# Layer B's queries by a seven-product block scheme, with the first tokens' z, k and v ahead of them

## The chip, the cores and the metric

The kernel runs on one core of one Trainium2 chip. A core has TensorE (PE, matmuls; PEld is its weight loads), VectorE (DVE), ScalarE (ACT), GpSimd (POOL) and SyncE (SP, which here issues most DMAs). The metric is the device time of one execution in microseconds, as the median of several runs.

## The reference

A hybrid decoder of two layers on 1024 tokens of width 1024, all in float32. Layer A is a gated MLP in chunks; layer B is sliding-window attention with 16 query heads, 4 key and value heads, ALiBi and sinks. Cut to what layer B computes:

```python
kv_in = rms_norm(h, kv_norm_g)
k_shared = (kv_in @ w_k).reshape(bsz, s_len, N_KV_HEADS, HEAD_DIM)
v_shared = (kv_in @ w_v).reshape(bsz, s_len, N_KV_HEADS, HEAD_DIM)
q, z = jnp.split(rms_norm(h, b_pre_g) @ w_in, 2, axis=-1)
q = q * (HEAD_DIM ** -0.5)
# per block of 128 queries: logits against the block's and the previous block's keys, + alibi, masked
m = jnp.maximum(jnp.max(logits, axis=-1), sink)
p = jnp.exp(logits - m[..., None])
denom = jnp.sum(p, axis=-1) + jnp.exp(sink - m)
o = jnp.einsum('bkgts,bskd->btkgd', p, vb) / denom
y = (o * jax.nn.silu(z)) @ w_out
h = h + rms_norm(y, b_post_g)
```

## The kernel before

**Numbers in two parts.** Each float32 operand of a large matmul is split into a high part in fp32r and a low part, the difference (`split` and `split_scaled`, L104 to L110): ACT writes the high part, DVE the low one. `mm3` (L168) then makes three matmuls: high by high, high by low, low by high. A product of one 128x128 weight tile with 512 tokens is thus three PE instructions, on L169 to L171.

**Stages.** The first tokens are 0 to 511 (h = 0), the second 512 to 1023 (h = 1). In order of time: the v layer of A; its u and z (`uz_layer`, the tiles ub, uc, ua, uz_slots); its output (`out_layer`); then layer B from L1204 on. A's three matrix products are already computed as seven block products for eight, with tiles T[1] to T[7] for the token side.

**Layer B.** q of the first tokens is computed first (`q_phase`, 8 output tiles of 128 by 8 tiles of K, in two passes of four PSUM banks), with the end of A for the second tokens (`chain_a`) as side work. Then k and v (`kv_phase`), with the transposes of the second tokens beside them (`norm_h1`); then z (`z_phase`). The first attention is `attn(0, ...)`: eight units (a block of 128 queries by half of the heads), each with two groups of scores (L1050), maximum (L1055, L1061), exponentials (L1065), normalising (L1070, L1071), transposes (L1078, L1079), causal selects on POOL (L1082, L1083), the product with v (L1097, L1099) and the gate (L1103). Between these, at four places for each unit, it draws steps from a generator of other PE work, the fill: 64 steps of k, v, q and half of z for the second tokens. A step is six matmuls of 512 columns, or their like. The second attention is filled with the other half of z and the output projections (`out_b0`, `out_b1`).

**Weights.** One object (`Weights`, L112) holds the order of all of layer B's weight tiles. A tile is loaded two steps ahead into one of three raw buffers by SP, and split one step ahead (L109 on ACT, L110 on DVE) into one of two pairs.

**What sets the order.** The framework orders each engine's instructions: program order is the priority, and an instruction goes when its operands and buffers are expected to be free. Waits are put in by it. Each DMA queue works in the order of issue.

**Other lines that matter below.** `broadcast_rstd` (L272) makes the token scale with two float32 matmuls on L278, from diagonal tiles. The first weight is loaded on ACT's queue (L406), behind the gains (L87). `evac` in `q_phase` (L971, L972) scales q out of PSUM and splits it into two half tiles.

## Time and profile before

| | |
|---|---|
| median of 3 runs | 1051.75 us (1051.14 to 1052.2) |
| the profiled execution | 1051.56 us, span 1049.8 us |
| instructions | 13661, of these 4994 matmuls |
| granted TensorE clock | 0.998 |
| HBM read, written | 125.21 MB, 31.46 MB |

The span is what the profile covers, from the first instruction to the last; the execution's own time holds 1.8 us more around it. A row of instructions gives the line, the engine, the operation, output and inputs by tile name, shape and count, then busy time, the mean of one in ns, and the idle time before it with what ended it. A row of the timeline begins with its start and its duration.

### The profile page before, as it was taken

What the parts mean: (1) busy time and instruction counts of PE and PEld (TensorE: products, weight loads), DVE (VectorE), ACT (ScalarE), POOL (GpSimd) and SP (SyncE); (2) the same over time, 40 slices, a digit from 0 to 9 for tenths busy, and PEclk for the clock granted to TensorE, in tenths of its full rate; (3) what the DMA queues carried; (4) which work ended last, traced back from release to release, by engine and by line L of the source; (5) the groups of instructions that cost most, each with busy time, mean ns of one, the idle gap of its engine ahead of it and who ended that gap; (6) DMA issues with size and microseconds to landing.
All of it is one profiled execution on the core that took longest, in us unless ns stands there. A gap on an engine that the chain in (4) does not pass through costs nothing.

```text
span 1049.8 us, 13661 instructions
## 1 busy us (share of the span) xinstructions
PE 1039.2 (99%) x4994; PEld 854.8 (81%) x4994; DVE 731.9 (70%) x1244; ACT 577.2 (55%) x989; POOL 195.2 (19%) x153
## 2 busy tenths in 40 slices
PE   9999999999999999999999999999999999999997
PEld 7888788888888888888888888888888777877776
DVE  6997466867768668677697587665247776667763
ACT  6683444555465565555444464654466665786631
POOL 0300003253342542530200000100001111011120
PEclk9999999999999999999999999999999999999999
DMA  8877252334333333347897642532222121211363
GB/s 310 271 282 269 101 177 88 116 105 143 124 121 116 132 124 117 108 137 272 322 352 270 201 160 93 200 102 86 95 81 71 51 81 61 81 61 61 121 220 120
DMA packets 80899, 157.56 MB, mean 150 GB/s; under 512 B 5824, under 2 KB 32704, under 8 KB 80832
## 3 DMA queue, kind: packets, MB, share of 16 engines
q1 hardware_dynamic: 76176, 147.75, 41.2%
q10 hardware_dynamic: 4656, 8.94, 2.4%
q8 instruction: 39, 0.64, 0.3%
q14 instruction: 28, 0.23, 0.1%
HBM read 125.21 MB, written 31.46 MB: 149 GB/s over the span
## 4 chain that ended last, share of the span: by engine, by line
PE 93%; DVE 4%; ACT 1%; issue 0%; DMA 0%; POOL 0%; DVEq 0%; POOLq 0%; ACTq 0%
PE ob L169 6%; PE ub L169 6%; PE ub L171 6%; PE ob L171 6%; PE ob L170 6%; PE ub L170 6%; PE qz L169 5%; PE qz L171 5%; PE qz L170 5%; PE uc L169 3%; PE uc L171 3%; PE uc L170 3%; PE s L1050 3%; PE sp L614 3%; PE vb L170 2%; PE vb L171 2%
## 5 line engine op out<-in xcount | busy, mean ns | idle before, releaser
L110 DVE SCALAR_TENSOR_TENSOR wlo<-raw_w,gn,whi 128x512 fp32r<-128x512 f32 x80 | 58.7, 758 | 62.2 <-ACT whi L109 62.0
L169 PE MATMUL qz<-n_hi,whi 128*128 128x512 f32 x256 | 101.0, 394 | 0.4 <-DVE q_lo L972 0.4
L171 PE MATMUL qz<-n_hi,wlo 128*128 128x512 f32 x256 | 100.0, 391 | 1.2 <-DVE wlo L110 1.2
L170 PE MATMUL qz<-n_lo,whi 128*128 128x512 f32 x256 | 99.8, 390 | 0.0
L109 ACT ACTIVATE whi<-raw_w,gn 128x512 fp32r<-128x512 f32 x80 | 54.9, 716 | 54.2 <-PE qz L170 35.0
L1065 ACT ACTIVATE pr<-pr,mx 128x129 f32<-128x129 f32 x128 | 50.0, 393 | 40.1 <-DVE mx L1061 40.0
L169 PEld LDWEIGHTS qz<-n_hi,whi 128*128 128x128 f32 x256 | 48.0, 188 | 16.6 <-issue 6.5
L105 ACT ACTIVATE uzhilo_g<-f 128x1024 fp32r<-128x1024 f32 x31 | 32.9, 1060 | 48.6 <-PE uc L171 42.7
L171 PEld LDWEIGHTS qz<-n_hi,wlo 128*128 128x128 f32 x256 | 48.0, 188 | 12.3 <-DVE wlo L110 2.1
L170 PEld LDWEIGHTS qz<-n_lo,whi 128*128 128x128 f32 x256 | 48.1, 188 | 9.3
L106 DVE TENSOR_TENSOR uzhilo_g<-f,uzhilo_g 128x1024 fp32r<-128x1024 f32 x31 | 39.0, 1257 | 19.9 <-ACT uzhilo_g L105 19.9
L209 ACT ACTIVATE uz_slots<-ub 128x512 f32<-128x512 f32 x48 | 28.3, 590 | 42.4 <-PE ub L171 39.0
L169 PE MATMUL ub<-T,whi_g 128*128 128x512 f32 x128 | 50.7, 396 | 0.0
L169 PE MATMUL ub<-T,uzhilo_g 128*128 128x512 f32 x128 | 50.5, 395 | 0.0
L171 PE MATMUL ub<-T,wlo_g 128*128 128x512 f32 x128 | 49.9, 390 | 0.0
L171 PE MATMUL ub<-T,uzhilo_g 128*128 128x512 f32 x128 | 49.9, 390 | 0.0
L170 PE MATMUL ub<-T,uzhilo_g 128*128 128x512 f32 x128 | 49.8, 389 | 0.0
L170 PE MATMUL ub<-T,whi_g 128*128 128x512 f32 x128 | 49.8, 389 | 0.0
L169 PE MATMUL uc<-T,uzhilo_g 128*128 128x512 f32 x124 | 48.9, 395 | 0.0
L170 PE MATMUL uc<-T,uzhilo_g 128*128 128x512 f32 x124 | 48.3, 389 | 0.0
L171 PE MATMUL uc<-T,uzhilo_g 128*128 128x512 f32 x124 | 48.3, 389 | 0.0
L105 ACT ACTIVATE whi_g<-raw_uz 128x1024 fp32r<-128x1024 f32 (+1 forms) x31 | 26.5, 854 | 36.7 <-PE ub L170 15.6
(332 smaller groups left out, 3071.4 us busy)
## 6 DMA issues: line engine op xcount, KB each, us to landing
raw_uz<-in_wuz_in_dram SPq DMA_DIRECT2D x32, 512.0 KB, 3.4
raw_w<-in_wqz_dram SPq DMA_DIRECT2D x32, 512.0 KB, 3.5
td<-uz_slots SPq DMA_DIRECT2D x56, 256.0 KB, 2.2
orawP2a<-td SPq DMA_DIRECT2D x28, 512.0 KB, 4.0
raw<-in_wv_in_dram SPq DMA_DIRECT2D x17, 512.0 KB, 4.8
vg<-vd SPq DMA_DIRECT2D x8, 1024.0 KB, 5.4
orawP2b<-in_wo_a_dram SPq DMA_DIRECT2D x16, 512.0 KB, 7.7
vraw<-in_wv_in_dram SPq DMA_DIRECT2D x13, 512.0 KB, 4.4
```

The lines of the kernel that those rows point to most:

```text
L105: nc.scalar.activation(hi, src, AF.Copy)
L106: nc.vector.tensor_tensor(lo, src, hi.bitcast(F32), ALU.subtract)
L109: nc.scalar.activation(hi, src, AF.Copy, scale=g)
L110: nc.vector.scalar_tensor_tensor(lo, src, g, hi.bitcast(F32), ALU.mult, ALU.subtract)
L169: nc.tensor.matmul(out, lhsT=a_hi, rhs=b_hi, start=start, stop=False, skip_group_check=True)
L170: nc.tensor.matmul(out, lhsT=a_hi, rhs=b_lo, start=False, stop=False, skip_group_check=True)
L171: nc.tensor.matmul(out, lhsT=a_lo, rhs=b_hi, start=False, stop=stop, skip_group_check=True)
L209: nc.scalar.activation(out, a, AF.Copy)
L614: nc.tensor.matmul(psv[:, n], lhsT=d["vg"][:, 4 * j + n, i * P:(i + 1) * P], rhs=d["wc"], start=True, stop=True)
L1050: nc.tensor.matmul(pss[par][:, g, w0:256], lhsT=q[par][:, m, bs_], rhs=w[par][:, p, ks], start=g + k == 0, stop=g + k == 2, skip_group_che ...
L1065: nc.scalar.activation(pr[:, i], pr[:, i], AF.Exp, bias=mx[:, i:i + 1], scale=-1.0, accum_out=dn[:, i:i + 1])
```

## The change

- **q in seven products.** The 1024 output channels of q are four groups of 256. Per group the weight is a 2 x 2 of blocks (two output tiles by two halves of K), the tokens a 2 x 2 (two halves of K by first and second tokens). Seven products of 12 matmuls each (4 tiles of K by three parts) replace eight, for both halves of the tokens at once. The token sums T[4] to T[7] are formed in `norm_sums`, beside z, k and v of the first tokens, which now come first. Products 1 and 2 of all four groups (`early_products`) need the first tokens alone; then come products 6, 5, 7, 3 and 4 of each group (`late_products`), with the weight sums in `prep1`.
- **Through DRAM.** The memory for this (pool `qp`) is that of attention, which is opened later. So z, k and v of the first tokens, the scaled weights and all of q are stored to DRAM (`zd`, `kd`, `qwd`, `qd`) and loaded again; q is split after the reload (`reload_q`), piece by piece, a step after its load (`reloads`).
- **Attention.** q is no longer fill. The first attention has 32 steps, six of them ahead of it (`first=6`, then 26). Half of the normalising goes to POOL, as four instructions of 128x128 for each unit.
- **Elsewhere.** `broadcast_rstd` uses fp32r in two parts, four matmuls; the first load moves to SP's queue, ahead of the x tiles; q of the first tokens takes tile P3, so the last output weights take P3 too.

The diff, cut to its core:

```diff
-            self.order += q + kv + z + kv + q + z
+            self.order += z + kv + kv + z
...
-            dg = sum_tile(f"dg{h}")[:, 0:512].rearrange("p (a b) -> p a b", a=4)
+            dg = st.tile([P, 2, 4, P], F32R, tag="xt", name=f"dg{h}")
             for j in range(4):
-                nc.vector.tensor_scalar(dg[:, j], ident, rx[h][:, j:j + 1], None, ALU.mult)
+                r = rx[h][:, j:j + 1]
+                nc.scalar.activation(dg[:, 0, j], ident, AF.Copy, scale=r)
+                nc.vector.scalar_tensor_tensor(dg[:, 1, j], ident, r, dg[:, 0, j].bitcast(F32),
+                                               ALU.mult, ALU.subtract)
             ps = bank("s", f"bc{h}")
-            nc.tensor.matmul(ps, lhsT=ones, rhs=dg.rearrange("p a b -> p (a b)"), start=True, stop=True)
+            for i in range(2):
+                nc.tensor.matmul(ps, lhsT=ones_r, rhs=dg[:, i].rearrange("p a b -> p (a b)"),
+                                 start=i == 0, stop=i == 1)
...
+        r0 = raws.take("v0")
+        load(r0[:, 0:512], wv_in[0, 0][:, 0:512])
         xload(xa[:, 0], 0, 0, 0, 1)
-        r0 = raws.take("v0")
-        nc.scalar.dma_start(out=r0[:, 0:512], in_=wv_in[0, 0][:, 0:512])
...
+    def norm_sums(n, yo, first):
...
+                split(n[0][:, ks, ts_], n[1][:, ks, ts_], ps)
+                if kq == 0:
+                    add(t1, ps, n_0[0][0][:, :, ts_].bitcast(F32), ALU.subtract)
+                    add(t1, t1, n_0[1][0][:, :, ts_].bitcast(F32), ALU.subtract, nc.gpsimd)
+                else:
+                    add(t3[:, :, ts_], ps, n[0][:, 0:HT, ts_].bitcast(F32), ALU.subtract)
+                    add(t2, ps, t1, ALU.subtract)
+                    add(t4, n_0[0][1][:, :, ts_].bitcast(F32), t2, ALU.subtract, nc.gpsimd)
+                    add(t3[:, :, ts_], t3[:, :, ts_], n[1][:, 0:HT, ts_].bitcast(F32), ALU.subtract, nc.gpsimd)
+                    add(t4, t4, n_0[1][1][:, :, ts_].bitcast(F32), ALU.add, nc.gpsimd)
+                yield
+            for m, src in ((5, t1), (6, t2)):
+                split(T[m][0][:, :, ts_], T[m][1][:, :, ts_], src)
+                yield
+            split(T[4][0][:, :, ts_], T[4][1][:, :, ts_], t4)
+            yield
...
+        def early_products(self):
+
+            for q in range(4):
+                self.prep_early(q + 1)
...
+                b = bank("mm", f"qa{q}")
+                self.product(q, 1, b, True, False)
+                self.p1[q] = sum_512(1 + q // 2, f"qp1_{q}")
+                copy(self.p1[q], b)
+                self.product(q, 2, b, False)
+                c = self.slot()
+                copy(c, b)
+                self.store(q, 0, 0, c)
+                yield
...
+        def late_products(self, side):
...
+                self.prep2(q)
+                self.load(q + 1)
...
+                step(side)
+                self.product(q, 6, b, True, False)
+                add(c01, p1, b, ALU.add)
+                self.product(q, 5, cc, True, False)
+                self.product(q, 7, b, False, False)
+                self.prep1(q + 1)
...
+                add(c11, p1, b, ALU.add)
+                add(c11, c11, cc, ALU.add)
+                self.store(q, 1, 1, c11)
+                self.product(q, 3, cc, False)
+                add(c01, c01, cc, ALU.add)
+                self.store(q, 0, 1, c01)
...
+                self.product(q, 4, b, False)
+                add(c10, p1, b, ALU.add)
+                self.store(q, 1, 0, c10)
...
+    def reload_q(q, i, r):
+
+        ms = slice(2 * i, 2 * i + 2)
+        for par in range(2):
+            rw, ot = half[par], half[1 - par]
+            g = qsc[rw, i // 2:i // 2 + 1]
+            nc.scalar.activation(q[par][rw, ms], r[rw], AF.Copy, scale=g)
+            nc.vector.scalar_tensor_tensor(q[par][ot, ms], r[rw], g, q[par][rw, ms].bitcast(F32),
+                                           ALU.mult, ALU.subtract)
...
+            if gp == 1:
+                nc.vector.reciprocal(dn[:, 0:4], dn[:, 0:4])
+                for i in range(4):
+                    nc.gpsimd.tensor_scalar(pr[:, i, 0:P], pr[:, i, 0:P], dn[:, i:i + 1], None, ALU.mult)
...
-            dn, pv = self.dn, self.pr[:, :, 0:P]
+            dn, pv = self.dn[:, 4:8], self.pr[:, 4:8, 0:P]
...
+    drain(qt.early_products())
+    q0, q1 = pair("P3", "q0"), None
+    side = reloads(0, None, None, 0, 1, None, 2, 3)
+    qt.late_products(side)
+    qp_ctx.close()
+    bp = ctx.enter_context(tc.tile_pool(name="bp", bufs=1))
...
+    reload_kv(qt.k0)
+    for i in range(4):
+        nc.sync.dma_start(out=z0[i // 2][:, i % 2 * 2:i % 2 * 2 + 2], in_=zd[i])
...
+    fill = chain(kv_phase(1, n1), z_phase(1, n1, z1, 0, 4))
+    attn(0, q0, z0, fill, 26, first=6,
+         side=chain(side, reloads(1, 0, 1)))
```

More of the change, by code (lines that the diff above doesn't have):

```diff
@@ L130, in split @@
         def split(self, i):
-            while len(self.done) <= min(i, len(self.order) - 1):
+            while len(self.done) <= min(i, self.limit - 1):
                 n = len(self.done)
@@ new lines, in reload_q, with reloads @@
+    def reload_q(q, i, r):
[6 more added lines that the diff above has]
+                                           ALU.mult, ALU.subtract)
+    def reloads(h, *pieces):
+        r = None
+        for i, p in enumerate(pieces + (None,)):
+            last = r
+            if p is not None:
+                r = raw_tile(f"q{h}_{p}").rearrange("p (m t) -> p m t", m=2)
+                nc.sync.dma_start(out=r, in_=qd[h][p])
+            if i and pieces[i - 1] is not None:
+                reload_q((q0, q1)[h], pieces[i - 1], last)
+            yield
@@ L979, in evac, with z_phase @@
+    def z_phase(h, n, z, m0, m1, keep=False):
         def evac(m, ps):
@@ L1104, in values, with attn @@
             split(q[0][:, ms, bs_], q[1][:, ms, bs_], yt)
-    def attn(h, q, z, fill, total, late=0):
+    def attn(h, q, z, fill, total, late=0, first=0, side=iter(())):
         taken = [0, 0]
+        for _ in range(first):
+            step(fill)
         n = 34 if late else 40
@@ L1123, in attn @@
             more()
+            step(side)
             if 0 <= i - 1 < len(units):
@@ new lines, in tile_yoco @@
+    main = chain(z_phase(0, n0, z0, 0, 8, keep=True), kv_phase(0, n0))
+    qt = QTiles()
+    step(main, main)
+    for i, _ in enumerate(main):
+        if i < 6 or i % 5 != 1 and i % 5 != 3:
+            step(side)
+        if i == 38:
+            qt.load_early(0)
+            qt.load_early(1)
+        elif i == 42:
+            qt.prep_early(0)
+            qt.load_early(2)
+    gp = post_gain(b_post, "gpb")
+    drain(side)
+    drain(qt.early_products())
+    q0, q1 = pair("P3", "q0"), None
@@ L1230, in tile_yoco @@
     fill = chain(z_phase(1, n1, z1, 4, 8), tail())
-    attn(1, q1, z1, fill, 48, 2)
+    attn(1, q1, z1, fill, 48, 2, side=reloads(1, 2, 3))
     drain(fill)
```

244 lines of the change are left out of this document (179 added, 65 removed).

## The prediction

> **What bounds the kernel now.** I read the page first: the busy times, then the chain that ended last.
>
> ```profile
> PE 1039.2 (99%) x4994; PEld 854.8 (81%) x4994; DVE 731.9 (70%) x1244; ACT 577.2 (55%) x989; POOL 195.2 (19%) x153
> ...
> PE 93%; DVE 4%; ACT 1%; issue 0%; DMA 0%; POOL 0%; DVEq 0%; POOLq 0%; ACTq 0%
> ```
>
> TensorE (PE) is busy 99% of the span and is 93% of the chain. A busy PE is not PE at its peak, since the matmuls overlap, so I read its price per matmul from the starts in the timeline: a product removed is worth its pitch, not its duration.
>
> Then the windows, cut at the stages around the change (start:end, length, then busy time and count of PE, PEld, DVE, ACT and POOL, granted clock, DMA share, GB/s). 654 to 699 is q of the first tokens, 699 to 726 their k and v, 726 to 769 their z, 769 to 892 the first attention; the first row is a piece of the v layer.
>
> ```profile
> 20.00:62.00 42.00, 41.66 (x183) 33.79 (x182) 40.90 (x48) 28.07 (x39) 10.20 (x3) 1.00 0.75 257
> ...
> 654.00:684.00 30.00, 28.88 (x127) 23.25 (x125) 21.95 (x32) 18.34 (x32) 3.82 (x3) 1.00 0.51 178
> ...
> 699.00:726.00 27.00, 27.00 (x182) 24.80 (x181) 17.26 (x27) 14.65 (x26) 0.00 (x0) 1.00 0.26 79
> 726.00:769.00 43.00, 43.00 (x192) 35.58 (x191) 14.21 (x21) 19.88 (x31) 0.00 (x0) 1.00 0.30 98
> 769.00:892.00 123.00, 122.56 (x669) 97.45 (x668) 90.63 (x254) 78.91 (x212) 15.29 (x14) 1.00 0.20 65
> 892.00:997.00 105.00, 105.00 (x547) 81.64 (x546) 72.38 (x222) 73.28 (x199) 16.15 (x14) 1.00 0.25 81
> ```
>
> PE fills each of these stages to within 1.2 us. In the first attention it can, because q of the second tokens is fill there: VectorE (DVE) has 90.6 us of work, but 123 us to do it in. That cover is what the change takes away.
>
> **The matmuls removed.** The timeline of PE in the present q gives the pitch; 54 matmuls lie between these two rows:
>
> ```profile
> 654.10 0.39 PE L169 MATMUL qz<-n_hi,whi 128*128 128x512 f32 x1
> ...
> 666.34 0.39 PE L169 MATMUL qz<-n_hi,whi 128*128 128x512 f32 x1
> ```
>
> (666.34 - 654.10)/54 = 0.2267 us. q is now 2 x 8 x 8 x 3 = 384 matmuls of this shape. Afterwards it is 4 groups x 7 products x 4 k x 3 = 336. So 48 x 0.2267 = **10.9 us** less, all on the path. The Trainium skill's page "TensorE: Matmul & The Clock Gate", section "Back-to-back issue gap", gives about 131 ns for a sustained matmul of 512 columns with its weight load; by that the 48 would be worth an estimated 6.3 us. The trace does not agree, and its pitch decides.
>
> **Smaller gains.** The broadcast of rstd, the start of the kernel, and three PE waits behind q's evacuation:
>
> ```profile
> 105.92 1.88 PE L278 MATMUL bc<-dg,ones 128*128 128x512 f32 x4
> ```
> ```profile
> 0.80 0.86 SPq L307 DMA_DIRECT2D xa<-in_xT_dram  x2
> ...
> 1.24 0.45 ACTq L406 DMA_DIRECT2D raw_v<-in_wv_in_dram  x1
> ...
> 5.78 1.24 POOL L415 CAST whi_v<-raw_v 128x512 fp32r<-128x512 f32 x2 [5.28 <-DMA raw_v<-in_wv_in_dram]
> ```
> ```profile
> 682.57 0.50 PE L171 MATMUL qz<-n_hi,wlo 128*128 128x512 f32 x1 [0.66 <-DVE wlo L110]
> ...
> 684.12 0.51 PE L171 MATMUL qz<-n_hi,wlo 128*128 128x512 f32 x1 [0.59 <-DVE wlo L110]
> ...
> 836.47 0.48 PE L169 MATMUL qz<-n_hi,whi 128*128 128x512 f32 x1 [0.45 <-DVE q_lo L972]
> ```
>
> The broadcast's two float32 matmuls show as four passes of 1.88 us together; four passes in fp32r at 0.227 are 0.91: **1.0 us** gained. The first load is issued 0.44 us after SP's first, behind the gains on ACT's queue; first on SP's it lands up to that much earlier, at the cost of the x loads, which it delays by as much; between 0 and 0.44 I take **0.4**, since the row after it waits for exactly this load. The three waits (0.66 + 0.59 + 0.45 = **1.7 us**) go with the work that jams DVE there. Gains: 10.9 + 1.0 + 0.4 + 1.7 = 14.0 us.
>
> **Waits inside the products.** An early group adds its second product to the bank from which ACT has just to copy the first; a late group's product 3 goes into the bank that DVE reads only after product 7, in two additions. PE waits if nothing else is at hand. The copies and additions from PSUM now cost:
>
> ```profile
> L209 ACT ACTIVATE uz_slots<-ub 128x512 f32<-128x512 f32 x48 | 28.3, 590 | 42.4 <-PE ub L171 39.0
> ...
> L206 DVE TENSOR_TENSOR uz_slots<-uz_slots,uc 128x512 f32<-128x512 f32 x32 | 22.0, 687 | 18.5 <-PE uc L171 11.3 <-ACT uz_slots L209 6.8
> ```
>
> With some 0.25 us for the last matmul's end, uncovered that is 4 x (0.59 + 0.25) = 3.4 us early and 4 x (2 x 0.69 + 0.25) = 6.5 us late: 9.9 us. The lower bound is 0. The order on PE is not the program's: here fill is put between the matmuls of one score, which the program issues together:
>
> ```profile
> 803.20 0.28 PE L1050 MATMUL s<-kh,q_hi 128*128 128x256 f32 x1
> ...
> 803.31 0.39 PE L169 MATMUL qz<-n_hi,whi 128*128 128x512 f32 x1
> ...
> 806.08 0.28 PE L1050 MATMUL s<-kl,q_hi 128*128 128x256 f32 x1
> ```
>
> So the next group's product, whose weights are split a group ahead, can be put into such a gap. I take **1.5 us**, near the lower end, by these rows.
>
> **z, k and v with the sums beside them.** Per block of tokens there are three more subtractions and three more splits on DVE, 24 in all, and 16 instructions on POOL:
>
> ```profile
> L106 DVE TENSOR_TENSOR n_lo<-nt,n_hi 128x512 fp32r<-128x512 f32 x8 | 5.1, 685 | 0.7 <-ACT n_hi L105 0.7
> ```
> ```profile
> L206 POOL TENSOR_TENSOR uz_slots<-uz_slots 128x512 f32<-128x512 f32 x17 | 27.7, 1631 | 0.5
> ```
>
> 24 x 0.685 = 16.4 us of DVE go into 70 us of PE, where the windows from 699 to 769 show DVE at 31.5 of 70; POOL gets 16 x 1.63 = 26 us. Both fit; I take nothing. Without that cover it would be the splits' waits, some 0.6 us each as in the two rows at 682 and 684.
>
> **From the last product to the first score.** Keys' tiles lie on memory that the products free last. The chain: addition 0.69, store of the last block, memset of kl, then four copies and a split of k; on SP the reloads of z and v (2.5 MB) and q's pieces stand ahead of the second tokens' third weight.
>
> ```profile
> td<-uz_slots SPq DMA_DIRECT2D x56, 256.0 KB, 2.2
> ```
> ```profile
> L1013 POOL MEMSET kl<- 64x2048 f32 x2 | 4.0, 2008 | 22.8 <-DVE ohiloP0b L106 19.1 <-DVE hb L763 3.8
> ```
> ```profile
> L1017 ACT ACTIVATE kh<-pk 64x512 fp32r<-64x512 f32 x4 | 2.4, 594 | 0.6 <-PE pk L171 0.5
> ```
>
> 0.69 + 2.2 + 2.0 + 4 x 0.59 = 7.3 us in a row, against six steps of fill put first, 6 x 6 x 0.227 = 8.2 us. Covered it costs 0; with ACT's queue full (eight copies, 4.7 us, and a weight's split) some 4 us. I take **1.0**.
>
> **The first attention with half its fill.** PE: 122.6 - 192 x 0.2267 = 79.0 us. DVE, from the groups of 769 to 892:
>
> ```profile
> L110 DVE SCALAR_TENSOR_TENSOR wlo<-raw_w,gn,whi 128x512 fp32r<-128x512 f32 x32 | 23.9, 772 | 13.9 <-ACT whi L109 13.9
> ...
> L1071 DVE TENSOR_TENSOR pr<-pr,dn 128x1024 f32<-128x1024 f32 x8 | 9.8, 1224 | 0.2
> ...
> L972 DVE SCALAR_TENSOR_TENSOR q_lo<-qz,qsc,q_lo 64x512 fp32r<-64x512 f32 x8 | 6.0, 755 | 1.2 <-ACT q_lo L971 1.0
> L972 DVE SCALAR_TENSOR_TENSOR q_hi<-qz,qsc,q_hi 64x512 fp32r<-64x512 f32 x8 | 5.8, 742 | 1.3 <-ACT q_hi L971 1.1
> L106 DVE TENSOR_TENSOR q_lo<-z,q_hi 128x512 fp32r<-128x512 f32 x8 | 5.5, 690 | 3.4 <-ACT q_hi L105 3.4
> ...
> L1019 DVE TENSOR_TENSOR kl<-pk,kh 64x512 fp32r<-64x512 f32 x4 | 2.8, 688 | 0.5 <-ACT kh L1018 0.4
> L1070 DVE RECIPROCAL dn<-dn 128x8 f32<-128x8 f32 x8 | 1.6, 203 | 6.0 <-ACT pr L1065 6.0
> ```
> ```profile
> L753 DVE SCALAR_TENSOR_TENSOR yoa<-yoa,rpa,xa 128x1024 f32<-128x1024 f32 x4 | 5.0, 1283 | 2.3 <-POOL rpa L179 1.2 <-DMA xa<-in_x_dram 1.1
> ```
>
> Of 90.6 us go 16 weight splits (12.4), q's evacuation (6.0 + 5.8) and half of the normalising (4.9). There come eight more reciprocals (1.6), four pieces of q with two instructions of 1024 columns each (8 x 1.28 = 10.3) and the first tokens' kl (2.8). That makes 76.2 us.
>
> Not all run at these durations. Half of the normalising goes to POOL, and q's low half, which had one input in PSUM, now has both in SBUF. In the layer where POOL works most, this is what DVE's instructions with two SBUF inputs and with one in PSUM take (min/median/max):
>
> ```profile
> L206 DVE TENSOR_TENSOR uz_slots<-uz_slots,bc x48: 679/688/1512, 171.6 to 499.1; 128x512 f32<-128x512 f32 x48
> ...
> L206 DVE TENSOR_TENSOR uz_slots<-uz_slots,sp x32: 674/681/689, 191.9 to 488.8; 128x512 f32<-128x512 f32 x32
> ```
> ```profile
> L206 DVE TENSOR_TENSOR uz_slots<-uz_slots,bc 128x512 f32<-128x512 f32 x48 | 38.7, 806 | 0.8
> ```
>
> The first kind is at times held for over twice its median and has a mean of 806 ns against 688 (+17%), the second kind never. The Trainium skill's page "SBUF — State Buffer", section "Who interferes with whom", says that a VectorE instruction with two SBUF inputs contends for a shared port with a GpSimd instruction that reads SBUF, and that the later one is blocked until the earlier one ends. The trace agrees, with those 1512 against 689 ns.
>
> In the first attention such instructions are what is left of the splits (12.4), the reloads (10.3), the normalising (4.9) and q_lo (5.5): 33 us, and 17% of them is 5.6. DVE: 81.8 us, more than PE's 79.0. The highest share that DVE held for long with PE nearly unhurt is 40.90 of 42 us (0.974, the first window). 81.8/0.974 = 84.0, so PE waits 84.0 - 79.0 = **5.0 us**. Below, it can be 0: PE may take the last z from the second attention, where DVE has 33 us free. Above, see the third rival. POOL's own part of the normalising, 32 instructions of 128x128, is a shape that the trace does not show; nearest are these:
>
> ```profile
> L1083 POOL TENSOR_SCALAR_AFFINE_SELECT pc<-pc 128x1024 f32<-128x1024 f32 x16 | 19.2, 1200 | 123.6 <-ACT pc L1079 122.6
> ...
> L586 POOL TENSOR_SCALAR_AFFINE_SELECT wc<-wc 128x128 f32<-128x128 f32 x8 | 10.5, 1317 | 47.4 <-DMA wc<-in_ws_t_dram 41.6 <-PE ub L171 5.8
> ```
>
> An eighth of 1.20 us and 1.32 us bound one: 5 to 42 us onto the stage's 15.3, under 79 either way, so POOL is no bound; near the upper end it holds DVE more often, which the third rival covers.
>
> **Sum.** 14.0 gained, 1.5 + 1.0 + 5.0 = 7.5 given back: 6.5 us faster. The profiled execution took 1051.56 (span 1049.8 and 1.8 around it): 1045.1. The median of the runs is 0.2 above it: **1045.3 us**.
>
> **Rivals.** *Everything hides* (chance 0.12): PE stays full because the order on PE fills each gap, as 803.20 shows; against it, DVE's 81.8 us. Time: 1051.75 - 14.0 = 1037.8. *The products' waits are not covered* (0.12): the gap filler needs the next group's weights, and ACT has eight scalings, a split and two copies for each early group; then 9.9 for 1.5, 1045.3 + 8.4 = 1053.7, no change that can be measured. *DVE sets the pace of the first attention at an ordinary share* (0.14), the case on the slower side: between 769 and 892 it reaches only 0.74 today, because additions, exponentials and copies wait for each other in turn; at 0.85 the stage takes 81.8/0.85 = 96.2, 17.2 us over PE, and the whole 1045.3 + 12.2 = 1057.5. It turns slower than before where the wait reaches 5.0 + 6.5 = 11.5 us, a share of 81.8/90.5 = 0.90. For it speaks that each step of attention leaves PE only 26/40 of a fill step at each of four places; against it, that PE may borrow fill. That the change does not do what it says has no room: 336 matmuls follow from the loops.
>
> **Numbers.** The forecast has 0.62. 0.2% (2.1 us) is about what a measurement of this kernel can tell from no change. Faster by more: forecast and the first rival, 0.74; the same: the second, 0.12; slower: the third, 0.14. The range goes from 1039.0, which leaves out the better half of the first rival, to 1053.0, which takes in the part of the second and third with half their waits and leaves out the rest, some 0.2 in all.
>
> **What would show it.** Right: 336 matmuls of q at a pitch near 0.227; bc's four near 0.9 us; in the first attention PE idle some 5 us, released by DVE, with DVE over 0.9 busy; reload instructions of mixed duration beside POOL; single PE waits under 1 us between products. Wrong: PE idle of a microsecond in each product with ACT or DVE as releaser (second rival), an attention of over 90 us (third), or PE idle elsewhere, above all for a weight's DMA behind the reloads.

## The result and the profile after

The changed kernel takes **1073.65 us** (median of 4 runs, 1073.09 to 1074.07) against 1051.53 for the kernel before in the same session: a ratio of 1.0213, with a 95% interval from 1.0201 to 1.0225. It is 22 us slower, and 28 us above the forecast of 1045.3. The profiled execution took 1074.07, with a span of 1072.3.

On the page of the kernel after, the lines for the engines, the chain and the costliest group:

```profile
PE 1039.2 (97%) x4946; PEld 847.7 (79%) x4946; DVE 767.3 (72%) x1282; ACT 601.2 (56%) x1054; POOL 283.9 (26%) x241
...
PE 77%; DVE 6%; POOL 6%; ACT 4%; DMA 3%; issue 3%; SPq 0%; DVEq 0%; POOLq 0%; ACTq 0%
...
L1261 POOL TENSOR_SCALAR pr<-pr,dn 128x128 f32<-128x128 f32 x64 | 46.3, 740 | 69.5 <-DVE dn L1259 58.4
```

The 48 matmuls are gone (4946 for 4994), yet PE is busy for the same 1039.2 us. The rows below show two reasons, which I did not add up: a matmul behind a wait overlaps with none before it, and some ran at a lower clock. PE's share of the chain fell from 93% to 77%, and POOL, DVE and ACT have entered it. POOL's 32 normalising instructions per attention now head the page's list of groups.

Next, windows cut at the first score and the first output product (`ob`), with columns as in the prediction. In the kernel before, from the first q matmul:

```profile
654.10:768.98 114.88, 113.63 (x562) 95.88 (x561) 59.60 (x85) 58.13 (x95) 3.82 (x3) 1.00 0.36 120
768.98:926.15 157.17, 156.72 (x849) 125.61 (x848) 110.74 (x326) 104.75 (x276) 17.47 (x16) 1.00 0.21 68
```

In the kernel after, from the first z matmul:

```profile
654.79:824.13 169.34, 158.55 (x759) 131.32 (x758) 106.25 (x128) 89.37 (x170) 41.31 (x28) 0.98 0.51 173
824.13:947.86 123.73, 111.93 (x604) 82.61 (x603) 101.19 (x321) 95.14 (x256) 49.30 (x60) 0.96 0.25 81
```

The forecast can be put on the same boundaries. z to score: 114.9 - 192 x 0.2267 + 336 x 0.2267 = 147.5, less the two old waits of 1.25, plus 2.5 of new waits, plus 8.2 for six fill steps put first: 157.0. Score to `ob`: 157.2 - 43.5 - 0.45 - 8.2 + 5.0 = 110.0.

| stretch, us | forecast | after | excess |
|---|---|---|---|
| start to the first z | 652.7 | 654.8 | 2.1 |
| first z to first score | 157.0 | 169.3 | 12.3 |
| first score to first `ob` | 110.0 | 123.7 | 13.7 |
| first `ob` to the end | 123.6 | 124.4 | 0.8 |

So the loss lies in two stretches of about equal size. The 2.1 us at the start are partly scatter: kernels that are the same up to the first z reach it between 653.83 and 655.25. The longer waits of PE in the two stretches, from the view of waits (engine, tile and line, whom it waited for: total, times, longest); none there is put down to a DMA:

```profile
PE qa L171 <- ACT kv L211: 6.3, 1, 6.3
PE o L1307 <- POOL pc L1293: 6.1, 2, 3.1
PE qb L171 <- DVE q_slots L208: 2.9, 1, 2.9
PE nt L792 <- DVE hb L783: 1.5, 1, 1.5
PE o L1307 <- DVE mx L1271: 1.4, 1, 1.4
PE o L1307 <- DVE pr L1244: 1.3, 1, 1.3
```

**The longest wait** is in front of the first early product. The timeline of all engines there, cut to what matters (start, length, instruction, and in brackets the idle time before it):

```profile
724.56 0.39 PE L173 MATMUL pk<-n_hi,wlo 128*128 128x512 f32 x1
...
724.65 0.61 ACT L105 ACTIVATE qT<-qt 128x512 fp32r<-128x512 f32 x1
...
725.18 2.25 POOL L208 TENSOR_TENSOR q_slots<-n_hi,qt 128x512 f32<-128x512 f32 x1
...
726.23 2.28 DVE L106 TENSOR_TENSOR wlo_q<-raw_qa,whi_q 128x1024 fp32r<-128x1024 f32 x1
...
727.51 2.12 POOL L208 TENSOR_TENSOR q_slots<-q_slots,n_lo 128x512 f32<-128x512 f32 x1
...
729.66 2.52 ACT L105 ACTIVATE qT<-q_slots 128x512 fp32r<-128x512 f32 x3 [4.40 <-POOL q_slots L208]
...
732.09 1.06 ACT L211 ACTIVATE kv<-pk 128x512 f32<-128x512 f32 x2
...
732.72 0.80 PE L171 MATMUL qa<-n_hi,whi_q 128*128 128x512 f32 x1 [6.34 <-ACT kv L211]
733.32 0.63 PE L172 MATMUL qa<-n_lo,whi_q 128*128 128x512 f32 x1
733.74 0.63 PE L173 MATMUL qa<-n_hi,wlo_q 128*128 128x512 f32 x1
```

Read it from below. PE waits for a bank that ACT frees by copying k. The last matmul of k (`pk`) had ended at 724.95, and ACT had nothing to do from 725.26 on, but its queue has a split of the last token block's sum ahead, and that waits 4.40 us for POOL. POOL's two additions take 2.25 and 2.12 us, while DVE's split beside them takes 2.28 us. For the three earlier blocks the same two additions took 1.74 to 1.75 and 1.62 to 1.63, with other DVE work beside them.

The last rows show a second price. The starts of the matmuls after the gap are 0.43 us apart, not 0.227, and the granted clock of these 10 us is 0.66:

```profile
730.00:740.00 10.00, 7.28 (x23) 5.76 (x24) 4.43 (x6) 8.86 (x23) 0.00 (x0) 0.66 0.51 203
```

The first ten matmuls after the gap take 4.37 us for 2.27. The gap cost 6.3 us, and the slow clock behind it 2.1 more.

**The first attention's longest waits** stand behind POOL. Here is its queue before the first of the two:

```profile
889.12 2.46 POOL L1261 TENSOR_SCALAR pr<-pr,dn 128x128 f32<-128x128 f32 x3 [3.00 <-PE s L1256]
...
891.54 1.48 POOL L1292 TENSOR_SCALAR_AFFINE_SELECT pp<-pc 128x1024 f32<-128x1024 f32 x1
...
893.00 0.60 POOL L1261 TENSOR_SCALAR pr<-pr,dn 128x128 f32<-128x128 f32 x1
...
893.56 1.09 POOL L1293 TENSOR_SCALAR_AFFINE_SELECT pc<-pc 128x1024 f32<-128x1024 f32 x1
...
894.71 1.98 PE L1307 MATMUL o<-pc,vt 128*64 128x512 f32 x4 [3.00 <-POOL pc L1293]
```

The two selects were ready when ACT's copy of the transposes ended at 889.23. They stand behind the normalising of the next unit: 2.46 us ahead of the first, 0.60 between the two, 3.06 together, against a wait of 3.00.

**The clock in the first attention.** PE is idle for 11.80 us of this stretch (123.73 - 111.93), 6.8 more than forecast. The other half of the 13.7 lies in PE's busy time. The granted clock fell three times:

```profile
860.00:862.00 2.00, 1.91 (x6) 0.85 (x6) 1.90 (x5) 1.95 (x6) 1.34 (x2) 0.50 0.00 0
894.00:896.00 2.00, 1.29 (x4) 0.55 (x6) 2.00 (x9) 0.00 (x0) 0.65 (x1) 0.51 0.52 184
908.00:910.00 2.00, 2.00 (x6) 0.66 (x8) 0.00 (x0) 0.13 (x1) 0.00 (x0) 0.50 0.03 9
```

The last two lie behind the two waits on the select, the first behind several shorter waits, of 1.30 us at most. A unit's eight matmuls for `o` take 1.87 us at full clock, from their first start (852.06) to the next instruction's, and 3.20 and 3.45 behind the two long waits. Together with the first place I estimate from the starts that the lower clock costs 4 to 5 us in this stretch.

### The profile page after: what moved, and what is told of

Read it like the earlier page. It is cut to its first block, busy times and chain, and to the rows that moved or that the text cites. A ratio compares the mean times of both kernels' runs of the same rounds, so it can differ in the third digit from the quotient of the medians.

```text
span 1072.3 us, 13875 instructions
## 1 busy us (share of the span) xinstructions
PE 1039.2 (97%) x4946; PEld 847.7 (79%) x4946; DVE 767.3 (72%) x1282; ACT 601.2 (56%) x1054; POOL 283.9 (26%) x241
## 4 chain that ended last, share of the span: by engine, by line
PE 77%; DVE 6%; POOL 6%; ACT 4%; DMA 3%; issue 3%; SPq 0%; DVEq 0%; POOLq 0%; ACTq 0%
PE ub L171 5%; PE ub L173 5%; PE ub L172 5%; PE ob L171 5%; PE ob L172 5%; PE ob L173 5%; PE uc L172 3%; PE uc L171 3%; PE uc L173 3%; PE sp L623 3%; PE vb L172 2%; PE vb L173 2%; PE vb L171 2%; PE oc L173 2%; PE oc L171 2%
## 5 line engine op out<-in xcount | busy, mean ns | idle before, releaser
L1261 POOL TENSOR_SCALAR pr<-pr,dn 128x128 f32<-128x128 f32 x64 | 46.3, 740 | 69.5 <-DVE dn L1259 58.4
L208 POOL TENSOR_TENSOR f<-raw_uz 128x512 f32<-128x512 f32 x15 | 20.2, 1347 | 126.2 <-DMA raw_uz<-in_wuz_in_dram 84.0
L208 POOL TENSOR_TENSOR f<-raw_uz,raw_uz 128x512 f32<-128x512 f32 x15 | 19.2, 1283 | 128.0 <-DVE uzhilo_g L106 128.0
L171 PE MATMUL z<-n_hi,whi 128*128 128x512 f32 x128 | 51.3, 401 | 0.5 <-DVE vt L1210 0.5
L110 DVE SCALAR_TENSOR_TENSOR wlo<-raw_w,gn,whi 128x512 fp32r<-128x512 f32 x48 | 37.9, 812 | 17.5 <-ACT whi L109 17.4
L172 PE MATMUL z<-n_lo,whi 128*128 128x512 f32 x128 | 50.4, 393 | 0.0
L173 PE MATMUL z<-n_hi,wlo 128*128 128x512 f32 x128 | 50.3, 393 | 0.0
L109 ACT ACTIVATE whi<-raw_w,gn 128x512 fp32r<-128x512 f32 x48 | 32.9, 716 | 28.1 <-PE qc L172 10.6
```

What stands on the lines that cost most here:

```text
L109: nc.scalar.activation(hi, src, AF.Copy, scale=g)
L110: nc.vector.scalar_tensor_tensor(lo, src, g, hi.bitcast(F32), ALU.mult, ALU.subtract)
L171: nc.tensor.matmul(out, lhsT=a_hi, rhs=b_hi, start=start, stop=False, skip_group_check=True)
L172: nc.tensor.matmul(out, lhsT=a_hi, rhs=b_lo, start=False, stop=False, skip_group_check=True)
L173: nc.tensor.matmul(out, lhsT=a_lo, rhs=b_hi, start=False, stop=stop, skip_group_check=True)
L208: (eng or nc.vector).tensor_tensor(out, a, b, op)
```

## The experiments

Each is described by its edit to the kernel after, if nothing else is said. The comparison is always with runs of the kernel before on the same chip (1051.17 to 1051.33). "Less than after" and "more" go across chips, on which the kernel before took 1051.17 to 1051.53. Lengths of a stretch come from one trace each. Line numbers in an experiment's rows are those of that kernel.

**The stretch of the products**

*Another bank for the early products.* If the bank alone holds them up, a bank of the other group frees them.

```
-                b = bank("mm", f"qa{q}")
+                b = bank("s", f"qa{q}")
```

> The changed kernel with the banks of the early products taken from the set that scores and transposes use, which is free there, so that they don't wait for ACT's copy of k. Theory B (PE's 6.3 us wait before the first early product is a wait for the bank, behind the token sums on POOL in ACT's queue): the wait shrinks to under 2 us and the clock is not lowered after it: 1065 to 1068. Rival O (the operands are late too): the wait keeps 4 us or more, 1071 to 1073.

Measured: 1075.11 us, ratio 1.0227 (1.0211 to 1.0242). The product starts earlier, and waits inside:

```profile
728.05 0.50 PE L173 MATMUL qa<-n_hi,wlo_q 128*128 128x512 f32 x1 [1.63 <-DVE wlo_q L106]
736.70 0.80 PE L171 MATMUL qa<-n_hi,whi_q 128*128 128x512 f32 x1 [5.18 <-ACT qp L211]
```

The wait has moved to ACT's next copy, qp, and is as long in sum (6.8 us). In ACT's queue qp stands behind the splits that wait 4.45 us for POOL, the copies of k and twelve scalings of weights (3.60 us). The bank is not the cause; what is late is ACT's queue.

*The block sums on DVE.* All four POOL additions of each token block, 16 in all.

```
-                    add(t1, t1, n_0[1][0][:, :, ts_].bitcast(F32), ALU.subtract, nc.gpsimd)
+                    add(t1, t1, n_0[1][0][:, :, ts_].bitcast(F32), ALU.subtract)
...
```

> The kernel after with the four block sums of each token tile that ran on POOL (L208, 16 instructions of 1.3 to 2.3 us) on DVE. Theory P (the last sums hold up ACT's queue, in which the copies of k stand, because POOL is slow and POOL and DVE hold each other up): the 6.3 us gap of PE at 726 to 732 falls below 2.5 us, the granted clock of that stage stays at 1.00, and the time falls by 5 to 9 us, to 1065 to 1069. Rival S (the stage has more vector work than fits, whichever engine does it; DVE stands at 9.9 and 9.3 of 10 us in 680 to 700 already): the gap stays at 5 us or more, or PE waits earlier in the stage, and the time is 1072 to 1077.

Measured: 1067.72 us, ratio 1.0151 (1.0134 to 1.0168), 5.9 less than after. The windows that had the gap:

```profile
720.00:730.00 10.00, 9.18 (x53) 7.75 (x52) 9.47 (x13) 8.55 (x20) 0.00 (x0) 1.00 0.60 214
730.00:740.00 10.00, 9.26 (x39) 7.35 (x40) 2.45 (x2) 5.06 (x10) 0.00 (x0) 1.00 0.73 259
```

PE is busy for 9.18 and 9.26 of 10 us where it was for 6.38 and 7.28, at full clock; what is left is one wait of 1.56 on qp. From the first z to the first score it takes 163.83 us for 169.34, and the stretch behind that is as long as in after (123.94). DVE takes the work though it gets almost full (9.47). POOL's slowness, together with ACT's queue behind it, was the cause.

*The sums earlier.* The side work steps four times in five, not three in five.

```
-        if i < 6 or i % 5 != 1 and i % 5 != 3:
+        if i < 6 or i % 5 != 1:
```

> The kernel after with the norm and block sums of the second tokens stepped four times in five steps of the z and kv products instead of three in five, so that they are issued some 8 steps earlier. Theory P (only the last token tile's sums come too late, DVE having 4.8 us free in 710 to 720): the gap of 6.3 us falls below 3 us and the time to 1066 to 1070. Rival S (DVE is full in 680 to 700, so what comes earlier pushes the weights' low parts back): PE waits 2 us or more on the weights' low parts within the z and kv products, and the time is 1071 to 1077.

Measured: 1075.15 us (1071.13 to 1076.38), ratio 1.0216 (1.0185 to 1.0248), not to be told from after. The gap of 6.3 us shrank to 1.37, but PE now waits within z and k:

```profile
692.55 0.50 PE L173 MATMUL z<-n_hi,wlo 128*128 128x512 f32 x1 [0.87 <-DVE wlo L110]
694.24 0.50 PE L173 MATMUL z<-n_hi,wlo 128*128 128x512 f32 x1 [0.72 <-DVE wlo L110]
720.05 0.50 PE L173 MATMUL pk<-n_hi,wlo 128*128 128x512 f32 x1 [1.60 <-DVE wlo L110]
```

These 3.2 us and two waits of 1.2 to 1.3 on qp take the gain back. By these waits each theory was half right: the gap was a matter of when the last block's sums come, and earlier there is no room on DVE for them and the weights' splits.

*PE kept busy in the gap*, with matmuls that nobody reads.

```
+    keep = bank("s", "keep")
+    for _ in range(24):
+        nc.tensor.matmul(keep[:, 0:P], lhsT=ones, rhs=ones, start=True, stop=True)
     drain(side)
     drain(qt.early_products())
```

> The kernel after with 24 matmuls of 128 columns, which nobody reads, between the kv products and the first early product. Theory C (the granted clock falls because PE stands idle for some us, and the work after the gap pays for it): with PE busy in the gap the clock of 730 to 740 is 0.95 or more instead of 0.66, the first qa matmul takes 0.4 instead of 0.8 us, and the time falls by 2 to 4 us, to 1069.5 to 1071.7, though the wait on ACT itself is as long. Rival L (the clock falls for another reason, and the gap's own length is the whole price): the clock stays near 0.66 or the time stays at 1073 to 1076, the added matmuls' own time being paid where they outlast the wait.

Measured: 1079.3 us, ratio 1.0264 (1.0248 to 1.0281), 5.6 more than after: a miss.

```profile
732.01 0.50 PE L171 MATMUL qa<-n_hi,whi_q 128*128 128x512 f32 x1 [0.88 <-ACT kv L211]
740.50 0.79 PE L171 MATMUL qa<-n_hi,whi_q 128*128 128x512 f32 x1 [4.56 <-ACT qp L211]
```

The first product did run at full clock (0.50 for 0.80 us, 0.98 for 0.66 in that window), as theory C has it for that place. But PE then waited 4.56 us on ACT's copy, and the clock fell there instead (0.68 in 740 to 750). ACT's queue shows why the copy came later than in after:

```profile
732.34 4.78 ACT L1036 ACTIVATE raw_qa<-raw_qa,gn 128x128 f32<-128x128 f32 x16
737.15 1.06 ACT L105 ACTIVATE whi_q<-raw_qa 128x1024 fp32r<-128x1024 f32 x1
738.90 1.06 ACT L105 ACTIVATE qhilo_q<-raw_qa 128x1024 fp32r<-128x1024 f32 x1 [0.69 <-DMA kd<-kv]
739.86 0.58 ACT L211 ACTIVATE qp<-qa 128x512 f32<-128x512 f32 x1
```

In after, twelve scalings stand ahead of qp; here they are sixteen and two splits. The edit moved ACT's order as well, so it does not isolate the clock, whose price stands on the starts above.

**The first attention**

*Half the normalising on POOL, alone*, in the kernel before, with all its cover.

```
+            if gp == 1:
+                nc.vector.reciprocal(dn[:, 0:4], dn[:, 0:4])
+                for i in range(4):
+                    nc.gpsimd.tensor_scalar(pr[:, i, 0:P], pr[:, i, 0:P], dn[:, i:i + 1], None, ALU.mult)
...
-            dn, pv = self.dn, self.pr[:, :, 0:P]
+            dn, pv = self.dn[:, 4:8], self.pr[:, 4:8, 0:P]
```

> The kernel before with half of the normalising on POOL, as in the change, and the fill left as it is. Theory P in its strong form (POOL's order hurts whatever the fill): 3 us slower or more. Theory PC (it hurts only where the fill is thin): within 1 us of 1051.5 in the first attention, whose fill is 64 steps.

Measured: 1052.64 us, ratio 1.0012 (1.0003 to 1.0022): 1.3 us, far from the 3 of the strong theory P.

*The thin cover, alone*, in the kernel before: q of the second tokens runs ahead of the first attention, which keeps 32 of its 64 fill steps.

```
+    drain(q_phase(1, n1, q1))
-    fill = chain(kv_phase(1, n1), q_phase(1, n1, q1), z_phase(1, n1, z1, 0, 4))
-    attn(0, q0, z0, fill, 64)
+    fill = chain(kv_phase(1, n1), z_phase(1, n1, z1, 0, 4))
+    attn(0, q0, z0, fill, 32)
```

> The kernel before with q of the second tokens computed ahead of the first attention in place of being its fill, 32 steps of fill for 64; no block products, nothing through DRAM, normalising on DVE. Theory C: the first attention gets 8 to 15 us of waits by itself, 1060 to 1066. Theory P: the thin fill alone costs under 3 us, 1052 to 1054.

Measured: 1058.05 us, ratio 1.0067 (1.005 to 1.0084): 6.7 us, between the two expectations, with the clock at 1.00 throughout the first attention. This is with eight products, no reloads and all normalising on DVE.

*Both together* in the kernel before.

> The kernel before with both changes of the first attention that were tried alone: q of the second tokens ahead of it, which leaves 32 steps of cover for 64 (alone +6.7 us), and half of the normalising on POOL (alone +1.3 us). If the two only add up: 1058.5 to 1060.5. If they multiply (POOL's longer way to the select and to the values matmuls is hidden by thick cover and bare under thin cover): 1062 to 1066, with waits of PE's o matmuls on the select of 2 us or more and a granted clock below 0.95 in some 10 us of the first attention.

Measured: 1059.6 us, ratio 1.0075 (1.0059 to 1.0091): 1.6 above thin cover alone. In the whole time they add up, as the first expectation has it.

*All normalising on DVE*, in the kernel after.

```
...
-                for i in range(4):
-                    nc.gpsimd.tensor_scalar(pr[:, i, 0:P], pr[:, i, 0:P], dn[:, i:i + 1], None, ALU.mult)
...
-            dn, pv = self.dn[:, 4:8], self.pr[:, 4:8, 0:P]
+            dn, pv = self.dn, self.pr[:, :, 0:P]
```

> The changed kernel with all of the normalising back on DVE, as before. Theory P (POOL's part of the normalising stands in the way of the causal selects, and PE waits for these at L1307): the two attentions lose the waits behind POOL, about 9 us of idle PE plus some of the time at a lower clock: 1060 to 1065. Theory C (the fill that was taken away is the cause, whatever POOL does): DVE gets 8 times 0.5 us more work in the first attention and the time stays within 3 us of 1073.7 or rises.

Measured: 1069.65 us, ratio 1.0173 (1.0157 to 1.0188), 4.0 less than after, between the two expectations. POOL's half costs 4.0 us here, for 1.3 and 1.6 in the kernel before. By stretches:

| us, one trace each | first score to first `ob` | first `ob` to the end |
|---|---|---|
| before | 157.17 | 123.65 |
| before, half on POOL | 157.18 | 124.83 |
| thin cover | 118.47 | 123.65 |
| thin cover, half on POOL | 119.86 | 124.77 |
| after, normalising on DVE | 119.03 | 123.45 |
| after | 123.73 | 124.44 |

In the last stretch POOL's half costs 1.0 to 1.2 us in all three pairs. Around the first attention it costs nothing under full cover and 4.7 in the changed kernel (5.1 with the sums on DVE). The 1.4 under thin cover cannot be told from scatter: after and four kernels that differ from it only ahead of this stretch take 121.85 to 124.55. So the sum of the whole times does not show that thin cover leaves POOL's price as it was. Which of the other differences (reloads beside it, six cover steps fewer) makes it dearer, no run separates.

*Both POOL edits undone*: sums and normalising on DVE.

> The kernel after with POOL taken out of both places: the four block sums of each token tile and all of the normalising on DVE. Alone these gave -5.9 and -4.0 us. If the two causes are separate (one holds up the products, the other the first attention): 1063 to 1065, with no gap of 3 us on POOL's select and the granted clock at 1.00 in 730 to 740. If they share the gain (DVE is too full for both): 1066 to 1069.

Measured: 1063.17 us, ratio 1.0111 (1.0096 to 1.0127), 10.5 less than after; the two gains add. PE's waits in the first attention are now

```profile
PE o L1303 <- DVE mx L1267: 4.3, 4, 2.3
PE pt L1284 <- DVE pr L1277: 2.7, 2, 1.5
PE s L1256 <- ACT pc L1285: 1.4, 1, 1.4
PE o L1303 <- POOL pc L1289: 1.4, 3, 0.7
PE z L171 <- DVE vt L1210: 0.4, 1, 0.4
```

They belong to the steps of a unit in turn: transposes wait for the normalising, scores for ACT's copy, values for a bank that DVE still reads or for the select. Three more experiments start from this kernel.

*Less DVE work*: the low part of eight weights is not computed, PE taking the high part in its place. These products then leave out the low part and count the high part twice, so only the time is of use.

```
+                thin = 12 <= n < 20
+                lo = hi if thin else wpool.tile([P, 1024], F32R, tag="wlo", name=f"wlo{n}")
...
+                        if thin:
+                            nc.scalar.activation(hi[:, cs], raw[:, cs], AF.Copy, scale=g)
```

> The kernel with sums and normalising on DVE (1063.2), and the low parts of the eight weights that are used in the first attention (k, v and half of z of the second tokens) not computed: PE takes the high part in their place, so the matmuls are as many and as long and these products are less exact. It takes 16 DVE instructions of 0.77 us, 12.4 us, off DVE, none of them in the chain from scores to values. Theory D (the amount of DVE work sets the pace of the first attention once its cover is thin): its PE waits of 9.8 us fall to 4 us or less and the time falls by 5 to 9 us, to 1054 to 1058. Rival L (each unit's chain of scores, maximum, exponential, normalising, transposes and select is too long for the cover, whatever DVE does beside it): 1061 to 1063.5.

Measured: 1060.34 us, ratio 1.0087 (1.0072 to 1.0102): 2.8 us for 12.4 us of DVE, between the two expectations. From the first score to `ob` it takes 115.45 us for 118.88.

```profile
PE pt L1293 <- DVE pr L1286: 3.2, 2, 2.4
PE o L1312 <- DVE mx L1276: 1.9, 1, 1.9
PE o L1312 <- POOL pc L1298: 1.8, 3, 0.9
```

The same in the kernel before with thin cover only:

> The kernel before with q of the second tokens ahead of the first attention (32 cover steps for 64, 1058.05), and the low parts of the eight weights used in that attention not computed, PE taking the high part in their place (the products are less exact, the matmuls as many). Nothing else of the change is in it. Theory D: 12.4 us less on DVE take away most of the 6.7 us that thin cover costs: 1052.5 to 1055. Rival L: 1056.5 to 1058.5.

Measured: 1056.21 us, ratio 1.0046 (1.0031 to 1.0061): 1.8 us of 6.7, just under the rival's range. So the amount of work on DVE explains about a quarter here, and less than theory D needs in both. The units' own chains are left as the larger part; that is argued from what is left and from the waits, and no run shortens a chain.

*The second tokens' q reloaded between the attentions*, first with the sums on DVE alone:

```
-         side=chain(side, reloads(1, 0, 1)))
+         side=side)
...
-    attn(1, q1, z1, fill, 48, 2, side=reloads(1, 2, 3))
+    late_r = reloads(1, 0, 1, 2, 3)
+    step(late_r, late_r, late_r)
+    attn(1, q1, z1, fill, 44, 2, first=4, side=late_r)
```

> The kernel with the sums on DVE (1067.7), and the reload of the second tokens' q, first two parts (DVE L1151 1.3 to 1.5 us each, and ACT's copies), taken out of the first attention and done between the two. Theory D (the reloads are one of the loads that make the first attention's vector chain late): the stage from the first score to the first output product loses 3 to 6 us, of which the place between the attentions takes back 1 to 3, so 1063 to 1067. Rival (the reloads fall where DVE is free): the stage keeps its length, and the time is 1067.5 to 1071.

Measured: 1072.64 us, ratio 1.0203 (1.0189 to 1.0217), 4.9 more and above both expectations. DVE had less to do, and PE's waits on the select rose to 11.8 us:

```profile
PE o L1307 <- POOL pc L1293: 11.8, 5, 3.5
```

The framework had put POOL's instructions in another order than without the edit. With all normalising on DVE the same edit gives:

> The same kernel (1063.2) with the first two parts of the second tokens' q reloaded between the two attentions, not in the first. When this was tried with half of the normalising on POOL it cost 4.9 us, all in waits on POOL's select. Theory D, with POOL out of the chain: the first attention loses four DVE instructions of some 1.4 us, its waits fall by 2 to 5 us, and the place between takes back 1 to 3: 1060 to 1064. Rival L: nothing falls in the first attention, and the place between costs 1 to 4: 1064 to 1067.

Measured: 1061.94 us, ratio 1.0098 (1.0083 to 1.0113), 1.2 less than without it; the two intervals overlap. By stretches this is what theory D expected: from the first score to `ob` it takes 3.4 us less (115.45), and 1.8 more behind that (125.17 for 123.39). So the reload does not cost the 4.9 us. They stand in waits behind POOL's normalising; that POOL's order alone brought them is not shown.

*The same 26 cover steps elsewhere.* Six kept back for the last two rounds (sums on DVE, normalising as in after):

```
-    attn(0, q0, z0, fill, 26, first=6,
+    attn(0, q0, z0, fill, 20, 1, first=6,
```

> The kernel with the sums on DVE (1067.7), and of the 26 cover steps of the first attention six kept back for its last two rounds, where no scores run and PE waited 3.0 and 3.1 us on POOL's select. Theory F (how thin the cover is at a place sets the wait there, and the lowered clock follows the long waits): these two waits fall below 1.5 us together with their lowered clock, the earlier ones grow by less, and the time falls by 2 to 5 us to 1063 to 1066. Rival W (the attention's vector chain sets the pace; cover moved is only a wait moved): 1066.5 to 1069.

Measured: 1073.46 us, ratio 1.0211 (1.0195 to 1.0227), 5.7 more and above both expectations; the waits on the select became five, of 11.2 us. And spread over the first 34 of 40 places, with all on DVE:

```
-        n = 34 if late else 40
+        n = 34
```

> The same kernel (1063.2) with the 26 cover steps of the first attention spread over its first 34 of 40 places and not over all, so denser at the start, where most of its waits are (6.9 of 9.8 us before 856). Theory F (the amount of cover at a place sets the wait there): the early waits fall by 2 to 3 us, the last two units wait 1 to 2 more: 1061 to 1063. Rival (the waits only move, or the new order brings others, as when six steps were kept back, which cost 5.7 us): 1063.5 to 1067.

Measured: **1058.33 us**, ratio 1.0067 (1.005 to 1.0084), 4.8 less, more than theory F expected. From the first score to `ob` it takes 114.89 us for 118.88.

```profile
PE pt L1284 <- DVE pr L1277: 3.0, 2, 1.5
PE o L1303 <- POOL pc L1289: 2.2, 4, 1.2
PE o L1303 <- DVE pr L1244: 2.2, 1, 2.2
```

The work of every engine is the same; only its place and order differ, and they move the time by as much as a POOL edit did.

**The small edits at the start**, in the kernel before:

> The kernel before with only the change's two small edits at the start: the token scale's broadcast as four matmuls of fp32r for two of fp32, and the first weight on SP's queue ahead of the x tiles. My sum had 1.0 and 0.4 us for them: 1049.9 (1049.3 to 1050.5) against 1051.3 if that holds. If the wait behind the broadcast or a later x tile takes it back: 1050.8 to 1051.8.

Measured over 11 runs: 1051.58 against 1051.27, ratio 1.0001 (0.9992 to 1.001). The broadcast's matmuls did get shorter, 1.07 us for 1.88 in the timeline, and nothing of it reaches the end.

**All that helped, in one kernel**: sums and normalising on DVE, reload between the attentions, cover over 34 places, or 28.

> All that helped so far in one kernel: sums and normalising on DVE, the cover spread over the first 34 of 40 places (alone -4.8 us), and the second tokens' first two parts of q reloaded between the attentions (alone -1.2 us). If the two add up: 1056.5 to 1058. If the reload's gain was a matter of where the cover stood: 1058 to 1061. In either case slower than the kernel before (1051.2): the products' stage still waits 5 us, and the attention's chains wait 6 to 8.

Measured: 1058.99 us, ratio 1.0075 (1.0058 to 1.0091), no better than the cover edit alone.

> The same with the cover spread over the first 28 of 40 places. Theory F (waits are set by the cover at a place) with an optimum still ahead: 1053 to 1056. If the last units are bare by then: 1058 to 1062, with waits of 2 us and more on the select from 880 on.

Measured: 1064.68 us, ratio 1.0124 (1.0109 to 1.0139), above both expectations. The units around 900 are bare then:

```profile
900.00:910.00 10.00, 6.07 (x24) 2.76 (x23) 7.46 (x16) 9.62 (x25) 2.18 (x2) 0.83 0.06 16
```

PE is busy for 6.07 of 10 us, behind one wait of 3.93 on the select, and the clock falls with it. No version with seven products came below the kernel before; the best stands 7 us above it.

## Why the prediction was wrong

- **Matmuls removed, 10.9 us: held.** 48 are gone, and where PE does not wait the pitch is still 0.227 (in the kernel with both POOL edits undone, 32 pitches from 784.92 to 792.17).
- **Broadcast and first load, 1.4 us: not there.** The matmuls' time fell by 0.8, the whole by nothing measurable; an early saving was not followed to the end.
- **The three waits behind q's evacuation, 1.7: gone.** One of 1.5 us on DVE's scaling of the second tokens (`hb`) stands in the same stretch in their place.
- **Waits inside the products, 1.5: too small.** The trace of after has one of 2.9 us there, behind an addition that stands in DVE's queue behind a late split; with the POOL edits undone there are 5.0 us in four waits, half of the second rival's 9.9. The interleaving that I had expected is there, without covering them all.
- **"Both fit; I take nothing" for the sums beside z, k and v: the first step that failed.** I read the room from the windows from 699 to 769 (DVE 31.5 of 70 us), where z, k and v stood before. The change moves them to 654 to 726, beside the end of A for the second tokens, where DVE had 45.5 of 72 us, q's work included; the sums stand behind that end of A in the same side work. In after DVE is busy for 9.90 and 9.30 us of the windows 680 to 690 and 690 to 700. As totals the sums still fit. But the last block's sums can start only when its transposes are done, near the end of the stretch, and they run in a row on POOL (2.25 and 2.12 us for the last two, where DVE takes 0.68), with ACT's queue waiting behind them and the copies of k in that queue. Undoing POOL's part gave 5.9 us. None of the rivals had this step.
- **Last product to first score, 1.0: held.** PE is full from 800 to 830.
- **First attention, 5.0: the second step that failed.** I divided DVE's work by a share that it holds elsewhere. The work itself came out: 110.74 - 90.63 + 81.8 = 101.9 us on the table's boundaries, 101.19 measured. But it does not set the length: taking 12.4 us of that work away gave 2.8 and 1.8 us, while moving cover without changing any engine's work gave between -4.8 and +5.7. A unit is a chain over PE, DVE, ACT and POOL, and its waits depend on what PE has to do at that place and on each engine's order; how much of the loss is the chain's own length stays open. POOL's half of the normalising, which I let pass because its total was far under 79 us, stands ahead of the select in POOL's queue: 4.0 us.
- **The third rival** (1057.5) came nearest. On the table's boundaries it gives 110.0 + 12.2 = 122.2 us for the first attention, and 123.73 were measured. The figure is in part luck: DVE's amount, by which it reckons, explains only the small part above, and 4.0 us are POOL's. Its reason, steps that wait for each other in turn, is what the waits show.
- **The clock was missing.** No term of the sum had a price for what follows a wait. Here it is a third of the longest one, 2.1 us, and by the estimate above 4 to 5 us more in the first attention.

Of the 22 us to the kernel before, 10.5 are the two POOL edits and 4.8 the place of the cover. The 7 us left are the net of 10.9 gained and some 18 lost. The thin cover alone is 6.7 of these. For the rest the trace shows PE's waits in the z and product stretch (5.4 us in the best version) and those that remain in the first attention, which no run took apart further.

## What to carry to other kernels

A stage's busy times say whether work fits, not whether it comes in time: for every piece that is moved beside a full PE, find the last one of its kind, and follow it through each engine's queue to what PE needs next. Take the busy times from the place where the work will run, not from where its cover runs now. A queue that works in order turns one slow instruction on a lightly used engine into a wait for all that stands behind it. Work that fills PE is worth more than its own time where chains run beside it, so taking it out has a price even when nothing is added.

## What the hardware showed

- **A wait can cost more than its length.** After 6.34 us of idle PE, ten matmuls ran at 0.43 us apart. The Trainium skill, "TensorE: Matmul & The Clock Gate", section "Part 1: The HAM clock gate", gives 426.7 ns for 512 columns at the gated clock and says that the gate closes after an idle window of about 3.4 us that runs freely. The trace agrees on the pitch and not on the length. In the kernel with early cover the matmul behind a wait of 2.11 us took 0.66 us, and the window from 770 to 780 had a clock of 0.84. In the one with all that helped, a wait of 2.12 us at the same place left the clock at 1.00, and in after one of 2.88 us did. And at 860 in after the clock fell to 0.50 with no single wait above 1.30 us. So the length of one wait does not tell here whether the clock falls.
- **POOL and DVE slow each other.** The same POOL addition took 1.74 to 1.75 us for three blocks and 2.25 for the fourth, beside a DVE split of 1024 columns, and that split took 2.28, against a mean of 1.26 for the 31 of that shape in the A layer of the kernel before.
- **Small instructions on POOL are dear.** A 128x128 scaling took 740 ns in the mean of 64. Eight of them, one unit of attention, would be 5.9 us; DVE scales the whole 128x1024 in 1.22.
